# Hymba step on one core: the opening of the first projection, x issued ahead of the small loads and scale and shift formed one channel tile at a time

## The chip, the core and the metric

The kernel runs on one core of a Trainium2 chip. A core has a matrix engine (PE), a vector engine (DVE), an activation engine (ACT), a general engine (POOL) and a synchronisation engine (SP) that here only issues transfers. PE writes its results to PSUM, of which this kernel has eight banks of 128 x 512 float32. Transfers run on 16 DMA engines, shared by the queues of SP, ACT and POOL.

The metric is device time in microseconds (us) of the whole program; the median of repeated runs is compared. The span of a profile is measured inside one execution and is a little shorter than that execution's device time.

## The reference

One transformer-like layer on 128 context tokens and 256 latent tokens of width 2048, in float32. What matters here is its first step:

```python
mod = silu(cond) @ ada_w + ada_b            # cond: c_ctx for the context, c for the latents
shift_a, scale_a, gate_a, shift_f, scale_f, gate_f = 6 parts of mod
h = rmsnorm(x, norm_w[0]) * (1 + scale_a) + shift_a
q, k, v, o, g, u = split(h @ w_in)          # width 4*1024 + 32 + 1024
```

After it come a bidirectional mLSTM and a pooling mixer, an output projection, and a squared-ReLU MLP. None of that is touched by the change.

## The kernel before

**Tiling.** The 384 tokens are three blocks of 128. The 2048 channels are 16 tiles of 128, and `h` is kept transposed, channels on partitions: tile `k` of `h` is `hh`, `hl` (the high and the low part of a float32 number, split so that three fast products replace one slow one). `x` is loaded as tokens on partitions (`xtok`, three transfers of 1 MB), and each channel tile is transposed by PE into a bank `xt` and copied to the SBUF tile `xT`, by ACT for odd `k` and DVE for even `k` (`transpose_x`, L399).

**First projection.** The loop of L481 runs over eight steps `s` of two channel tiles each, and in each step over five column chunks: `u` (two of 512 columns), `v` (384, 384, and 256 with the 32 gate columns). A chunk's weights are one transfer `raw`, split by ACT into `hi` (L134) and by DVE into `lo` (L135). A chunk takes three PSUM banks, one per token block, and 18 matmuls: two channel tiles, three blocks, three products (hi x hh, hi x hl, lo x hh). At step 0 the chunk `u` of columns 0 to 511 runs its products one kind after the other, over both channel tiles. After a chunk its three banks are copied out (L514) or added up (L516).

**Scale and shift.** `mod` comes from rows of `ada_w`, streamed through PE: `ada_mat` (L239) loads 512 KB slabs `ada_raw` and multiplies them by the silu of the conditioning vectors (`sg`, transposed as `cT`, L105 to L112); ACT copies the result to `ada_sb` (L268), PE turns it to channels on partitions (L272), DVE adds the bias and the norm weight (`ada_finish`). For channel tiles 0 and 1, scale and shift are one result of 256 columns each, four slabs each. The generator `first_ada` yields between slabs; `X_ORDER` (L417) interleaves it with the first transposes and with the broadcast of 1/rms (letter `b`: `dg_rx` on DVE, `bc_rx` on PE, `rbc` on DVE); `ADA_STEPS` says how many of its slabs follow each chunk of step 0. `make_h` (L436) forms `hm` (x times scale times 1/rms) on DVE, then `hh` on ACT and `hl` on DVE.

**1/rms.** ACT squares each token block in two halves with a running sum (`junk`, L388), behind the table load and the exponential of the silu (L108); then DVE, POOL and DVE make `rx`.

**What sets the order.** Up to the first projection the order on PE, DVE and ACT is that of the code (`manual_schedule`); in the loop it is so for PE alone, and DVE, ACT and SP take an order from the planner. Each transfer of SP and ACT takes the next of eight semaphores, `DMAHW0` to `DMAHW7`, and is issued only once the transfer that had this semaphore before has landed. Tiles are reused from pools: `ada` and `hi`/`lo` have four buffers each, `raw` three, and PSUM eight banks, so that an instruction that writes a buffer waits for the last reader of what lay there.

Of the kernel before, what the change touches and what calls it, by code (L numbers as in the profile page):

```python
# [13 lines left out]
P = 128  # L14
# [29 lines left out]
def hymba_kernel(  # L44
# [6 lines left out]
    nc = tc.nc  # L51
# [24 lines left out]
    pre = pre_scope.enter_context(tc.tile_pool(name="pre", bufs=1))  # L76
    prm = pre.tile([P, 2, P], F32, name="prm")
    masks = vp.tile([P, N_CST - 3, P], F32, name="masks")
    nc.scalar.dma_start(cc[:, 0, :], c_ctx.rearrange("(p j) -> p j", j=16))
    nc.scalar.dma_start(cc[:, 1, :], c[0].rearrange("(p j) -> p j", j=16))  # L80
    nc.scalar.dma_start(cst[:, 0:3], cs_src[:, 0:3])

    vsb = [vp.tile([P, NH, 129], F32, name=f"v{i}") for i in range(3)]
    gsb = vp.tile([P, 3, 32], F32, name="gsb")
    x_tok = [pre.tile([P, D], F32, tag=f"x{i}", name=f"xtok{i}") for i in range(3)]
    for t, src in zip(x_tok, (x_prompt[0], x_sample[0, 0:128], x_sample[0, 128:256])):
        nc.sync.dma_start(t, src)
    nc.scalar.dma_start(prm[0:96, 1, :], ada_b[0].rearrange("(r p) -> r p", p=P))
    nc.scalar.dma_start(prm[0:64, 0, :], norm_w[0].rearrange("i (k p) -> (i k) p", p=P))
    nc.scalar.dma_start(prm[64:72, 0, :], mlstm_norm_w[0].rearrange("(k p) -> k p", p=P))  # L90
    nc.scalar.dma_start(prm[72:80, 0, :], pool_scale[0].rearrange("(k p) -> k p", p=P))
# [299 lines left out]
    xT = []  # L391
# [7 lines left out]
    def transpose_x(k, later=False):  # L399
        ps = bank(f"xt_{k}")  # L400
        for i in range(3):
            nc.tensor.transpose(ps[:, i * P:(i + 1) * P], x_tok[i][:, k * P:(k + 1) * P], ident)
        t = slot(f"xT{k}")
        xT.append(t)

        def copy():
            if k % 2:
                nc.scalar.activation(t[:, 0:NTOK], ps[:, 0:NTOK], AF.Copy)
            else:
                nc.vector.tensor_copy(t[:, 0:NTOK], ps[:, 0:NTOK])  # L410

        if later:
            xt_late.append(copy)
        else:
            copy()
# [20 lines left out]
    def make_h(s, between=None):  # L436
        ts = []
        for k in range(ksteps[s][0], sum(ksteps[s])):
            t, hi, lo = slot(f"hm{k}"), slot(f"hh{k}", F32R), slot(f"hl{k}", F32R)
            ts.append((k, t, hi, lo))  # L440
            for g, (a, b) in enumerate(GROUPS):
                nc.vector.scalar_tensor_tensor(t[:, a:b], xT[k][:, a:b], mod[:, 1, k, g:g + 1], rbc[:, a:b], op0=ALU.mult, op1=ALU.mult)
        if between is not None:
            between()
        for k, t, hi, lo in ts:
            for g, (a, b) in enumerate(GROUPS):
                i1 = nc.scalar.activation(hi[:, a:b], t[:, a:b], AF.Identity, bias=mod[:, 0, k, g:g + 1])
# [17 lines left out]
    w_first = load_chunk(0, 0, later=lo_later)  # L465

    def shift_rows():
        for _ in range(2):
            transpose_x(len(xT), True)
        next(ada0)  # L470
        for _ in range(2):
            transpose_x(len(xT), True)

    h_ins = make_h(0, shift_rows)
    lo_later[0]()
    for copy in xt_late:
        copy()
    order.close()
    order2 = ExitStack()
    order2.enter_context(tc.manual_schedule(engines={mybir.EngineType.PE}))  # L480
    for s in range(NS):  # L481
        for ci, (kind, c0, w) in enumerate(chunks):
            k0, nk = ksteps[s]
            hi, lo, n = w_first if s == 0 and ci < 2 else load_chunk(s, ci, h_ins if s == 0 else ())
# [3 lines left out]
            acc = [bank(f"{kind}_{c0}_{s}_{i}") for i in range(3)]  # L488

            ways = ((0, 0), (1, 0), (0, 1))  # L490
            for ps in [ways[n:n + 1] for n in range(3)] if s == ci == 0 else [ways]:
                for k in range(nk):
                    for i in range(3):
                        for a, b in ps:
                            nc.tensor.matmul(acc[i][:, 0:n], h[k0 + k][a][:, i * P:(i + 1) * P], (hi, lo)[b][:, k, :],  # L495
                                             start=k == 0 and a + b == 0, stop=k == nk - 1 and b == 1)
                    if ci == 3 and k == 0:
                        next(ada0, None)
            if s == ci == 0:
                w_first = load_chunk(0, 1, h_ins)  # L500
            if s == 0 and ci == XT_AT:
                while len(xT) < KT:
                    transpose_x(len(xT))
            for _ in range((ADA_STEPS if s == 0 else (1, 1, 1, 0, 0))[ci]):
                next(ada0, None)
            if ci == 3 and s < NS - 1:
                make_h(s + 1)
# [881 lines left out]
```

## Time and profile before

| | us |
|---|---|
| median of 3 runs | 1687.03 (1686.95, 1687.03, 1689.38) |
| device time of the profiled execution | 1689.57 |
| span in its profile | 1687.9 |
| PE busy in the span | 1656.9 (98%) |
| first matmul of the projection | 28.71 after the span's start |

In the tables of stages each row is a stretch of the span, with the busy time of each engine, the granted clock of PE, the share of the DMA engines' time and their rate. In the timelines a row is a start, a duration, an engine, a line and an operation, and in brackets how long the engine had been idle and what ended that. `SPq` and `ACTq` are the engines' instruction queues as issuers of transfers. `q1` is SP's DMA queue, `q10` that of ACT, `q0` that of POOL; their rows give packets, MB and the share of 16 engines' time.

### The profile page before, as it was taken

What the parts mean: (1) busy time and instruction counts of PE and PEld (TensorE: products, weight loads), DVE (VectorE), ACT (ScalarE), POOL (GpSimd) and SP (SyncE); (2) the same over time, 40 slices, a digit from 0 to 9 for tenths busy, and PEclk for the clock granted to TensorE, in tenths of its full rate; (3) what the DMA queues carried; (4) which work ended last, traced back from release to release, by engine and by line L of the source; (5) the groups of instructions that cost most, each with busy time, mean ns of one, the idle gap of its engine ahead of it and who ended that gap; (6) DMA issues with size and microseconds to landing.
All of it is one profiled execution on the core that took longest, in us unless ns stands there. A gap on an engine that the chain in (4) does not pass through costs nothing.

```text
span 1687.9 us, 27859 instructions
## 1 busy us (share of the span) xinstructions
PE 1656.9 (98%) x10965; PEld 1582.5 (94%) x10965; DVE 1340.3 (79%) x2009; ACT 752.4 (45%) x1225; POOL 130.9 (8%) x181
## 2 busy tenths in 40 slices
PE   6999999999999999999999999999999999999997
PEld 4888999999999989989999999999999999999996
DVE  3677769898999959997797688988588488588688
ACT  4332355555443345543444444444444444444443
POOL 0000002221000024430000000000000000000120
PEclk9999999999999999999999999999999999999999
DMA  9999857777789964754546245544344443433653
GB/s 319 316 296 298 277 160 256 238 250 223 237 270 309 311 203 129 217 153 126 173 152 194 88 138 173 158 150 140 110 150 127 124 138 114 149 122 112 187 183 134
DMA packets 258195, 320.95 MB, mean 190 GB/s; under 512 B 14752, under 2 KB 223248, under 8 KB 257680
## 3 DMA queue, kind: packets, MB, share of 16 engines
q1 hardware_dynamic: 250256, 303.41, 57.0%
q0 software_dynamic: 5856, 13.69, 2.8%
q10 hardware_dynamic: 1952, 2.07, 0.4%
q8 instruction: 86, 1.41, 0.3%
q14 instruction: 45, 0.37, 0.1%
HBM read 308.61 MB, written 10.51 MB: 189 GB/s over the span
## 4 chain that ended last, share of the span: by engine, by line
PE 90%; DVE 4%; DMA 3%; issue 1%; SPq 1%; ACT 0%; POOL 0%; DVEq 0%; ACTq 0%; POOLq 0%
PE acc_w L144 10%; PE acc_w L143 10%; PE acc_w L145 10%; PE y L1223 4%; PE y L1224 4%; PE y L1222 4%; PE v L495 4%; PE u L495 3%; PE acc_wo L143 3%; PE acc_wo L144 3%; PE acc_wo L145 3%; PE y_yz L1223 2%; PE y_yz L1222 2%; PE y_yz L1224 2%; PE y L1066 2%; PE y L1065 2%
## 5 line engine op out<-in xcount | busy, mean ns | idle before, releaser
L144 PE MATMUL acc_w<-h2l,hi_w 128*128 128x384 f32 (+1 forms) x1024 | 346.2, 338 | 0.5 <-DVE h2l L1016 0.5
L143 PE MATMUL acc_w<-h2h,hi_w 128*128 128x384 f32 (+1 forms) x1024 | 344.2, 338 | 1.2 <-ACT h2h L1012 1.2
L145 PE MATMUL acc_w<-h2h,lo_w 128*128 128x384 f32 (+1 forms) x1024 | 345.1, 337 | 0.0
L135 DVE TENSOR_TENSOR lo_w<-raw_w,hi_w 128x1024 fp32r<-128x1024 f32 x152 | 185.3, 1221 | 137.0 <-ACT hi_w L134 136.8
L134 ACT ACTIVATE hi_w<-raw_w 128x1024 fp32r<-128x1024 f32 x152 | 160.8, 1058 | 215.2 <-PE acc_w L144 94.9
L316 DVE SCALAR_TENSOR_TENSOR ada_acc<-ada_raw,sg,ada_acc 128x1024 f32<-128x1024 f32 (+1 forms) x240 | 252.0, 1080 | 0.8 <-DMA ada_raw<-in_ada_w_dram 0.7
L143 PEld LDWEIGHTS acc_w<-h2h,hi_w 128*128 128x128 f32 x1024 | 192.2, 188 | 2.8 <-ACT h2h L1012 2.0
L144 PEld LDWEIGHTS acc_w<-h2l,hi_w 128*128 128x128 f32 x1024 | 192.6, 188 | 1.2 <-DVE h2l L1016 0.8
L145 PEld LDWEIGHTS acc_w<-h2h,lo_w 128*128 128x128 f32 x1024 | 192.4, 188 | 0.3 <-DVE lo_w L135 0.2
L1208 ACT ACTIVATE hi_t<-w 128x1024 fp32r<-128x1024 f32 x104 | 109.6, 1060 | 119.1 <-DVE w L1244 34.3
L1209 DVE TENSOR_TENSOR lo_t<-w,hi_t 128x1024 fp32r<-128x1024 f32 x104 | 126.3, 1220 | 15.1 <-ACT hi_t L1208 14.8
L1209 DVE TENSOR_TENSOR lo_b<-w,hi_b 128x1024 fp32r<-128x1024 f32 x78 | 95.3, 1221 | 41.9 <-ACT hi_b L1208 41.6
L1208 ACT ACTIVATE hi_b<-w 128x1024 fp32r<-128x1024 f32 x78 | 82.5, 1059 | 98.1 <-PE acc_w L144 66.7
L134 ACT ACTIVATE hi_wo<-raw_wo 128x1024 fp32r<-128x1024 f32 x32 | 34.0, 1064 | 80.6 <-DMA raw_wo<-in_w_out_dram 57.4
L942 ACT ACTIVATE z<-acc_w 128x384 f32<-128x384 f32 x54 | 26.3, 487 | 75.1 <-PE acc_w L145 75.1
L495 PE MATMUL v<-hi_v,hh 128*128 128x384 f32 (+1 forms) x144 | 48.0, 333 | 0.0
L134 ACT ACTIVATE hi_v<-raw_v 128x768 fp32r<-128x768 f32 (+1 forms) x24 | 19.0, 793 | 64.4 <-DMA raw_v<-in_w_in_dram 55.6
L495 PE MATMUL v<-lo_v,hh 128*128 128x384 f32 (+1 forms) x144 | 46.6, 324 | 1.0 <-DVE lo_v L135 1.0
L495 PE MATMUL v<-hi_v,hl 128*128 128x384 f32 (+1 forms) x144 | 46.5, 323 | 0.0
L135 DVE TENSOR_TENSOR lo_wo<-raw_wo,hi_wo 128x1024 fp32r<-128x1024 f32 x32 | 38.8, 1217 | 7.8 <-ACT hi_wo L134 7.0
L143 PE MATMUL acc_k<-hh,hi_k 128*128 128x384 f32 x128 | 44.2, 345 | 0.0
L143 PE MATMUL acc_o<-hh,hi_o 128*128 128x384 f32 x128 | 43.9, 343 | 0.0
(2264 smaller groups left out, 4549.0 us busy)
## 6 DMA issues: line engine op xcount, KB each, us to landing
raw_w<-in_w_dram SPq DMA_DIRECT2D x152, 512.0 KB, 4.2
ada_raw<-in_ada_w_dram SPq DMA_DIRECT2D x130, 512.0 KB, 4.7
w<-in_w_dram SPq DMA_DIRECT2D x104, 512.0 KB, 4.1
raw_wo<-in_w_out_dram SPq DMA_DIRECT2D x32, 512.0 KB, 5.1
u<-in_ada_w_dram SPq DMA_DIRECT2D x18, 512.0 KB, 6.6
raw_u<-in_w_in_dram SPq DMA_DIRECT2D x16, 512.0 KB, 7.0
raw_q<-in_w_in_dram SPq DMA_DIRECT2D x16, 512.0 KB, 4.8
raw_k<-in_w_in_dram SPq DMA_DIRECT2D x16, 512.0 KB, 4.9
```

Of the source, the lines that this page charges most:

```text
L134: nc.scalar.activation(hi[:, 0:n], raw[:, 0:n], AF.Copy)
L135: low = lambda: nc.vector.tensor_tensor(lo[:, 0:n], raw[:, 0:n], hi[:, 0:n].bitcast(F32), op=ALU.subtract)
L143: nc.tensor.matmul(ps, lh, rh, start=start, stop=False)
L144: nc.tensor.matmul(ps, lh, rl, start=False, stop=False)
L145: mm3.ins = nc.tensor.matmul(ps, ll, rh, start=False, stop=stop).ins
L316: nc.vector.scalar_tensor_tensor(acc[:, g, :], raw[:, a, :], cj, acc[:, g, :], op0=ALU.mult, op1=ALU.add)
L495: nc.tensor.matmul(acc[i][:, 0:n], h[k0 + k][a][:, i * P:(i + 1) * P], (hi, lo)[b][:, k, :], start=k == 0 and a + b == 0, stop=k == nk - 1 ...
L1208: nc.scalar.activation(hi, raw, AF.Copy)
L1209: nc.vector.tensor_tensor(lo, raw, hi.bitcast(F32), op=ALU.subtract)
L1222: nc.tensor.matmul(acc, xh, wh, start=start and j == 0, stop=False)
L1223: nc.tensor.matmul(acc, xh, wl, start=False, stop=False)
L1224: nc.tensor.matmul(acc, xl, wh, start=False, stop=stop and j == 3)
```

## The change

Four things are done.

1. The three `x` transfers stand ahead of everything else. ACT's queue then issues `cst` (identity, ones), `c_ctx` and `c`, in this order; the four `prm` transfers (bias and norm weights) move from ACT's queue to POOL's.
2. For channel tiles 0 and 1, scale and shift are formed one tile at a time: scale of tile 0, shift of tile 0, then scale and shift of tile 1. Each is a result of 128 columns with two slabs of 8 x 128 (512 KB as before, in pieces of 512 B instead of 1024 B).
3. `u`'s two chunks of step 0 take tile 0's products alone (9 matmuls each), by kind; then, after tile 1's scale and shift, tile 1's. The two chunks' six banks stay open between.
4. `X_ORDER` makes 7 transposes before the first product instead of 12 (with those inside `make_h`); 5 come before tile 1's products and 4 after them. `ADA_STEPS` changes from (4, 0, 4) to (3, 2, 3).

```diff
-XT_AT = 0
-ADA_STEPS = (4, 0, 4, 0, 0)
-X_ORDER = "tatatatattaatabata"
+ADA_STEPS = (3, 2, 3, 0, 0)
+X_ORDER = "ttatatabata"
...
-    nc.scalar.dma_start(cc[:, 0, :], c_ctx.rearrange("(p j) -> p j", j=16))
-    nc.scalar.dma_start(cc[:, 1, :], c[0].rearrange("(p j) -> p j", j=16))
-    nc.scalar.dma_start(cst[:, 0:3], cs_src[:, 0:3])
...
     for t, src in zip(x_tok, (x_prompt[0], x_sample[0, 0:128], x_sample[0, 128:256])):
         nc.sync.dma_start(t, src)
-    nc.scalar.dma_start(prm[0:96, 1, :], ada_b[0].rearrange("(r p) -> r p", p=P))
...
+    nc.scalar.dma_start(cst[:, 0:3], cs_src[:, 0:3])
+    nc.scalar.dma_start(cc[:, 0, :], c_ctx.rearrange("(p j) -> p j", j=16))
+    nc.scalar.dma_start(cc[:, 1, :], c[0].rearrange("(p j) -> p j", j=16))
+    nc.gpsimd.dma_start(prm[0:96, 1, :], ada_b[0].rearrange("(r p) -> r p", p=P))
...
             if k0 == 0:
-                yield from ada_mat([(1, k0, nk)])
-                yield from ada_mat([(0, k0, nk)], ("lo",))
+                for k in range(nk):
+                    yield from ada_mat([(1, k, 1)])
+                    yield from ada_mat([(0, k, 1)], ("lo",))
...
+    def shift_rows(before, behind, later):
+        for _ in range(before):
+            transpose_x(len(xT), later)
+        next(ada0)
+        for _ in range(behind):
+            transpose_x(len(xT), later)
+
+    def chunk_mm(acc, n, w, k0, ks, nk, by_way):
+
+        ways = ((0, 0), (1, 0), (0, 1))
+        for ps in [ways[m:m + 1] for m in range(3)] if by_way else [ways]:
+            for k in ks:
+                for i in range(3):
+                    for a, b in ps:
+                        nc.tensor.matmul(acc[i][:, 0:n], h[k0 + k][a][:, i * P:(i + 1) * P], w[b][:, k, :],
+                                         start=k == 0 and a + b == 0, stop=k == nk - 1 and b == 1)
+                yield
+
     lo_later = []
...
-    h_ins = make_h(0, shift_rows)
+    w_first = [load_chunk(0, 0, later=lo_later)]
+    h_ins = make_h([0], lambda: shift_rows(1, 1, True))
     lo_later[0]()
...
+    w_first.append(load_chunk(0, 1, h_ins))
+    acc_first = []
+    for ci in range(2):
+        kind, c0, w = chunks[ci]
+        acc_first.append([bank(f"{kind}_{c0}_0_{i}") for i in range(3)])
+        for _ in chunk_mm(acc_first[ci], w, w_first[ci], 0, [0], 2, True):
+            pass
+        for _ in range(2 if ci == 0 else 3):
+            next(ada0)
+        if ci:
+            h_ins = make_h([1], lambda: shift_rows(3, 2, False))
     for s in range(NS):
         for ci, (kind, c0, w) in enumerate(chunks):
...
+            acc = acc_first[ci] if early else [bank(f"{kind}_{c0}_{s}_{i}") for i in range(3)]
+            for k, _ in enumerate(chunk_mm(acc, n, (hi, lo), k0, [1] if early else range(nk), nk, early)):
+                if ci == 3 and k == 0:
+                    next(ada0, None)
+            if s == 0 and ci == 1:
                 while len(xT) < KT:
                     transpose_x(len(xT))
```

Three places show what moves. The first is SP's queue at the program's start, before:

```order
L87 DMA xtok0_89<-in_x_prompt_dram 128x2048
L87 DMA xtok1_90<-in_x_sample_dram 128x2048 [waits DMAHW0_49]
L87 DMA xtok2_91<-in_x_sample_dram 128x2048 [waits DMAHW1_49]
L252 DMA ada_raw_1_0_0_146<-in_ada_w_dram 128x4x256 [waits DMAHW2_49]
L252 DMA ada_raw_1_0_4_158<-in_ada_w_dram 128x4x256 [waits DMAHW3_49]
```

and with the change:

```order
L82 DMA xtok0_86<-in_x_prompt_dram 128x2048
L82 DMA xtok1_87<-in_x_sample_dram 128x2048
L82 DMA xtok2_88<-in_x_sample_dram 128x2048
L250 DMA ada_raw_1_0_0_152<-in_ada_w_dram 128x8x128
L250 DMA ada_raw_1_0_8_168<-in_ada_w_dram 128x8x128
L250 DMA ada_raw_0_0_0_195<-in_ada_w_dram 128x8x128 [waits DMAHW0_49]
```

The second and third `x` transfer and the first slabs no longer wait for a small load's semaphore. The second place is ACT at the same time, before (`cc` holds `c_ctx` and `c`, `sg` is the silu's exponential, `junk` the squares of `x`):

```order
L79 DMA cc<-in_c_ctx_dram 128x16
L80 DMA cc<-in_c_dram 128x16
L81 DMA cst<-in_consts_dram 128x384
L108 ACT_TABLE_LOAD [waits DMAHW2_49]
L108 ACTIVATE sg<-cc 128x32 [waits DMAHW0_49]
L388 ACTIVATE junk,ssq<-xtok_89 128x1024 [waits DMAHW1_49]
```

and with the change:

```order
L83 DMA cst<-in_consts_dram 128x384
L84 DMA cc<-in_c_ctx_dram 128x16
L85 DMA cc<-in_c_dram 128x16
L106 ACT_TABLE_LOAD [waits DMAHW3_49]
L106 ACTIVATE sg<-cc 128x32 [waits DMAHW2_49]
L387 ACTIVATE junk,ssq<-xtok_86 128x1024 [waits DMAHW1_49]
```

The table load and the squares stand behind `cc` in both; `cc` now stands behind `cst` in ACT's queue. The third place is PE around the transposes that come between products, the first matmul of each tile shown. Before, behind the last product of `u`'s first chunk:

```order
L495 MATMUL u_0_0_2_312<-lo_u_0_0_259,hh1_267 128x512
L402 MATMUL xt_12_337<-cst_72,xtok0_89 128x128 [waits PE_49]
L402 MATMUL xt_13_343<-cst_72,xtok0_89 128x128 [waits Activation_49]
L402 MATMUL xt_14_349<-cst_72,xtok0_89 128x128 [waits DVE_49]
L402 MATMUL xt_15_355<-cst_72,xtok0_89 128x128 [waits Activation_49]
```

and with the change, behind tile 0's products of both chunks:

```order
L477 MATMUL u_512_0_2_304<-lo_u_512_0_264,hh0_235 128x512
L401 MATMUL xt_7_345<-cst_72,xtok0_86 128x128 [waits DVE_49]
L401 MATMUL xt_8_351<-cst_72,xtok0_86 128x128 [waits Activation_49]
L401 MATMUL xt_9_357<-cst_72,xtok0_86 128x128 [waits DVE_49]
L401 MATMUL xt_10_365<-cst_72,xtok0_86 128x128 [waits DVE_49]
L401 MATMUL xt_11_371<-cst_72,xtok0_86 128x128 [waits Activation_49]
L477 MATMUL u_0_0_0_267<-hi_u_0_0_231,hh1_341 128x512 [waits Activation_49]
```

Nine transposes now stand behind the first product instead of four, while six of the eight banks hold `u`'s sums.

More of the change, by code (lines that the diff above doesn't have):

```diff
@@ L87, in hymba_kernel @@
         nc.sync.dma_start(t, src)
[L88 to L91 removed]
+    nc.scalar.dma_start(cst[:, 0:3], cs_src[:, 0:3])
+    nc.scalar.dma_start(cc[:, 0, :], c_ctx.rearrange("(p j) -> p j", j=16))
+    nc.scalar.dma_start(cc[:, 1, :], c[0].rearrange("(p j) -> p j", j=16))
+    nc.gpsimd.dma_start(prm[0:96, 1, :], ada_b[0].rearrange("(r p) -> r p", p=P))
+    nc.gpsimd.dma_start(prm[0:64, 0, :], norm_w[0].rearrange("i (k p) -> (i k) p", p=P))
+    nc.gpsimd.dma_start(prm[64:72, 0, :], mlstm_norm_w[0].rearrange("(k p) -> k p", p=P))
+    nc.gpsimd.dma_start(prm[72:80, 0, :], pool_scale[0].rearrange("(k p) -> k p", p=P))
     gbias = const.tile([P, 32], F32, name="gbias")
@@ L434, in hymba_kernel, with make_h @@
     chunks = [("u", 0, 512), ("u", 512, 512), ("v", 0, 3), ("v", 3, 3), ("v", 6, 2)]
-    def make_h(s, between=None):
+    def make_h(ks, between=None):
         ts = []
-        for k in range(ksteps[s][0], sum(ksteps[s])):
+        for k in ks:
             t, hi, lo = slot(f"hm{k}"), slot(f"hh{k}", F32R), slot(f"hl{k}", F32R)
@@ L462, in load_chunk @@
         return load_w(pieces, f"{kind}_{c0}_{s}", ksteps[s][1] * n, after, later) + (n,)
-    lo_later = []
[L465 to L472, printed above, removed]
-    h_ins = make_h(0, shift_rows)
+    def shift_rows(before, behind, later):
[7 more added lines that the diff above has]
+        for ps in [ways[m:m + 1] for m in range(3)] if by_way else [ways]:
+            for k in ks:
+                for i in range(3):
[3 more added lines that the diff above has]
+                yield
+    lo_later = []
+    w_first = [load_chunk(0, 0, later=lo_later)]
+    h_ins = make_h([0], lambda: shift_rows(1, 1, True))
     lo_later[0]()
@@ L483, in hymba_kernel @@
             k0, nk = ksteps[s]
-            hi, lo, n = w_first if s == 0 and ci < 2 else load_chunk(s, ci, h_ins if s == 0 else ())
+            early = s == 0 and ci < 2
+            hi, lo, n = w_first[ci] if early else load_chunk(s, ci, h_ins if s == 0 else ())
             if s == NS - 1 and ci == 4:
@@ L487, in hymba_kernel @@
                     nc.sync.dma_start(masks, cs_src[:, 3:N_CST])
[L488 to L501, printed above, removed]
+            acc = acc_first[ci] if early else [bank(f"{kind}_{c0}_{s}_{i}") for i in range(3)]
[3 more added lines that the diff above has]
+            if s == 0 and ci == 1:
                 while len(xT) < KT:
@@ L506, in hymba_kernel @@
             if ci == 3 and s < NS - 1:
-                make_h(s + 1)
+                make_h(range(ksteps[s + 1][0], sum(ksteps[s + 1])))
             for i in range(3):
```

## The prediction

> **What bounds the kernel now.** The page first: PE is busy for nearly the whole span, so time is won or lost where PE stands still or gets work that used to lie in a gap.
>
> ```profile
> span 1687.9 us, 27859 instructions
> ...
> PE 1656.9 (98%) x10965; PEld 1582.5 (94%) x10965; DVE 1340.3 (79%) x2009; ACT 752.4 (45%) x1225; POOL 130.9 (8%) x181
> ```
>
> Then the busy time by stage (stretch, its length, PE, PEld, DVE, ACT, POOL, clock, DMA share, GB/s). The change lies in the first 60 us.
>
> ```profile
> 0.00:10.00 10.00, 0.97 (x3) 0.47 (x3) 2.09 (x10) 3.66 (x6) 2.59 (x11) 1.00 0.74 231
> 10.00:20.00 10.00, 5.41 (x35) 2.27 (x35) 1.34 (x4) 5.12 (x10) 0.89 (x1) 1.00 1.05 367
> 20.00:30.00 10.00, 9.31 (x82) 5.42 (x80) 5.29 (x15) 4.93 (x11) 0.00 (x0) 1.00 1.08 358
> 30.00:40.00 10.00, 10.00 (x74) 7.38 (x73) 6.50 (x9) 5.89 (x11) 0.00 (x0) 1.00 0.99 322
> 40.00:50.00 10.00, 10.00 (x80) 8.61 (x79) 2.42 (x8) 6.08 (x12) 0.00 (x0) 1.00 1.05 344
> ```
>
> PE idles 14 us in the first 20 us and none from 30 to 50. The chain of waits says what the idle time is for, and what PE then does without a gap (start, length, what).
>
> ```profile
> 0.80 5.19 DMA cc<-in_c_ctx_dram
> ...
> 6.01 0.33 SPq L87
> ...
> 18.73 8.55 DMA raw_u<-in_w_in_dram
> ...
> 28.71 4.63 PE u L495 x18
> 33.34 1.31 PE xt L402 x12
> 34.65 1.97 PE ada L256 x32
> 36.62 4.39 PE u L495 x18
> 41.01 3.16 PE v L495 x18
> ...
> 47.82 0.34 PE ada L272 x4
> ```
>
> The second x transfer waits until 6.0 for the semaphore of `c_ctx`; all else queues behind it in one stream, and the first product starts at 28.71. Until then PE does twelve transposes and eight slabs of scale and shift in time that it had to wait anyway. Behind 28.71 every microsecond of PE work counts. PE's later waits up to 200 us are few:
>
> ```profile
> PE v L495 <- DVE lo_v L135: 1.0, 1, 1.0
> PE ada L272 <- ACT ada_sb L268: 0.8, 1, 0.8
> ```
>
> **The change, first part: when the first product starts.** x no longer waits, but the small loads now share the DMA engines with three x transfers instead of one. Two stretches of 1 us each, at 2.5 and 3.5, show how they share (packets, MB, share):
>
> ```profile
> q1 hardware_dynamic: 35, 0.29, 72.9%
> q10 hardware_dynamic: 35, 0.00, 2.3%
> ...
> q1 hardware_dynamic: 50, 0.41, 97.0%
> q10 hardware_dynamic: 49, 0.00, 3.4%
> ```
>
> One packet of ACT's queue passes for each 8 KB packet of x, about 3 per engine and us. Before, `c_ctx` and `c` were first in ACT's queue and x had one transfer. Now the queue holds `cst`, `c_ctx`, `c`: 8 data packets and a closing one per engine each, 27 in all, and the three x transfers have as many. So `c` lands about with the last of x. Each x takes 2.6 us (in the rows below ACT begins the second at 11.35 and the third at 13.94); issued from 0.81 on without a gap, the last lands near 12.0 where it was 13.9: my estimate, first x at 5.8 as now (issue 0.81, 5.0 to landing), two more at 2.6, and 1.0 for the small packets between them. `c` lands at 12.0 too, where ACT had it at 6.29. On ACT the table load and the exponential wait for `c`, and the squares of x stand behind them:
>
> ```profile
> 6.29 1.28 ACT L108 ACT_TABLE_LOAD   x1 [6.29 <-DMA cc<-in_c_dram]
> 7.59 0.23 ACT L108 ACTIVATE sg<-cc 128x32 f32<-128x32 f32 x1
> 7.72 1.04 ACT L388 ACTIVATE junk<-xtok 128x1024 f32<-128x1024 f32 x1
> ...
> 11.35 1.06 ACT L388 ACTIVATE junk<-xtok 128x1024 f32<-128x1024 f32 x1 [1.32 <-DMA xtok<-in_x_sample_dram]
> ...
> 13.94 1.06 ACT L388 ACTIVATE junk<-xtok 128x1024 f32<-128x1024 f32 x1 [0.25 <-DMA xtok<-in_x_sample_dram]
> ...
> 16.08 0.19 ACT L388 ACTIVATION_READ_ACCUMULATOR junk<-xtok 128x1 f32 x1
> ```
>
> Before, squares ran while x arrived and ended at 16.27. Now all six come after `c`: 12.0, plus 1.4 for table and exponential (6.29 to 7.72), plus three times 2.33 (13.94 to 16.27) is 20.4, 4.1 later. What follows, with its rows:
>
> ```profile
> 16.30 0.16 DVE L394 TENSOR_REDUCE ss<-ssq 128x3 f32<-128x6 f32 x1 [7.12 <-ACT junk L388]
> 16.57 0.55 DVE L410 COPY xT<-xt 128x384 f32<-128x384 f32 x1
> 17.50 0.49 ACT L408 ACTIVATE xT<-xt 128x384 f32<-128x384 f32 x1 [1.23 <-PE xt L402]
> 19.68 0.55 PE L402 MATMUL xt<-cst,xtok 128*128 128x128 f32 x3
> 23.50 0.55 DVE L206 TENSOR_TENSOR dg_rx<-cst,rx 128x384 f32<-128x384 f32 x1
> 24.10 0.91 PE L208 MATMUL bc_rx<-dg_rx,cst 128*128 128x384 f32 x2 [0.49 <-DVE dg_rx L206]
> 26.76 0.38 ACT L268 ACTIVATE ada_sb<-ada 128x256 f32<-128x256 f32 x1 [0.17 <-PE ada L256]
> 27.31 1.06 ACT L134 ACTIVATE hi_u<-raw_u 128x1024 fp32r<-128x1024 f32 x1 [0.17 <-DMA raw_u<-in_w_in_dram]
> 28.27 1.48 ACT L447 ACTIVATE hh<-hm,mod 128x128 fp32r<-128x128 f32 x4
> ```
>
> DVE stands in order: sum and scale 0.3, two copies 1.0 (both waited for nothing but the squares ahead of them in DVE's queue), scale of tile 0 0.4, `dg_rx` 0.55: 22.7. `bc_rx` 0.9: 23.6. PE has tile 0's shift behind it: two slabs of 0.5 (1.97 for four), a transpose 0.33 (1.31 for four), 0.3 until the last is through: 25.2. `ada_sb` 0.3, then on ACT `hi_u` 1.06 and the first `hh` 0.3, with hand-overs of 0.05 (`dg_rx` ends 24.05, `bc_rx` starts 24.10): 27.6. `raw_u` is no longer what ends last: 12.0 plus four slabs of 1.75 (a price from below) plus 1.4 is 20.4. So the first product starts at 27.6 instead of 28.71: **-1.1**, where the x transfers alone promised more. Lower bound: `c` as early as before, 21.9 (rival A). Upper bound: if `c` also waits for the first two slabs, 3.5 later, 31.1.
>
> The Trainium skill, "TensorE: Matmul & The Clock Gate", Part 1, says that an idle window of about 3.4 us halves the array's clock until it has been busy as long. PE would idle from about 16 to 21 here, while it waits for ACT behind the squares. Nothing in the rows quoted shows PE after such a gap; by the page's halving, the two slabs and the transpose (1.33 us) would take about 1.3 more, and the sum below would be +8.4 instead of +7.1, an estimate.
>
> **Second part: PE work that now stands behind the first product.** Tile 1's four slabs 1.97, two more turns of the result (L272, 0.34 for four records, 0.17 each) 0.34, and five more transposes (nine instead of four) at 0.33, 1.65. Together **+3.96**. The products themselves are the same 36 matmuls. A slab now has eight matmuls of 128 columns instead of four of 256; below, each costs half: no change; above, each costs as much as one of 256: +2.0. I take the lower: 18 products of 512 columns took 4.39, 18 of 384 took 3.16, so time goes with the columns.
>
> **Third part: PE waits that arise.** The sums of `u` hold six banks from the first product to the copies after tile 1, scale or shift holds a seventh, and one is left for transposes. So each transpose waits until the one before is copied out: 0.55 until it is through, 0.53 copy (ACT 0.49, DVE 0.55), two hand-overs, 1.18, of which PE works 0.33: 0.85 idle. That meets transposes 8 and 9 in full, 10 by half (0.4, a turn stands between), and 13, 14, 15 in full: 4.65. Transpose 11's copy stands on ACT ahead of tile 1's `hh`: 0.9 before tile 1's first product. Tile 0's third kind of product waits for `lo_u`, which DVE makes behind `hl`: 0.8 for `hl` and 1.2, against 1.4 for six products: 0.5. Together **+6.05**. Below: none of it if work fills the gaps, but PE's order is the code's, so nothing can step forward; I allow 3. Above, with a second ACT item ahead of each copy, 9.
>
> **Fourth part: what is given back.** At step 1 and 4 PE waits 1.0 and 0.8 for late weights; PE coming later, both should vanish: **-1.8**. The work behind is unchanged in PE's order.
>
> Cost nothing: `prm` on POOL (needed first at 21, by `ada_finish`), the reversed `cst` (first transposes wait for x), the number of slabs.
>
> **Sum:** -1.1 + 3.96 + 6.05 - 1.8 = +7.1. The profiled execution took 1689.57 around its span of 1687.9, and would take 1696.7; the median of the runs shown is 1687.03, 2.5 lower, so I predict 1694.1.
>
> **Rivals.** *A, the small loads are not held back.* `c` lands at 6.3; squares end 2.4 after x, and `raw_u` sets the start: 20.4 + 1.06 + 0.3 and hand-overs, 21.9, 5.7 earlier than forecast. PE then reaches the second slab of tile 1's shift at 28.3, which lands at 30.3 (four slabs, two `raw_u`, and one slab of 1.5 further down the stream), and waits 2.0. 7.1 - 5.7 + 2.0 = +3.4: 1690.4. For it: in the trace `c_ctx` needed 5.2 us beside one x. Against: the rows of 35 to 35 and 50 to 49.
>
> *B, transfers in 512 B pieces are slow.* Bounds from stretches at 6.1 to 6.5 (mostly the small loads' 512 B) and 13.5 to 15.5 (1024 B):
>
> ```profile
> q10 hardware_dynamic: 188, 0.08, 72.6%
> ...
> q1 hardware_dynamic: 751, 0.75, 108.3%
> ```
>
> 0.726 x 16 x 0.4 us / 188 is 25 ns a packet of 0.4 KB on average, and 1.083 x 16 x 2 / 751 is 46 ns for 1 KB. I take 27 ns, 64 per engine and slab, 1.75 us. At 46 a slab takes 2.9; six slabs later the second slab of tile 1's shift lands at about 40 where PE is at 34: +5.8, 1699.9.
>
> *C, not slower: the transfers, not PE, set step 1.*
>
> ```profile
> 62.55 0.45 PE L495 MATMUL v<-lo_v,hh 128*128 128x384 f32 x1 [1.02 <-DVE lo_v L135]
> ```
>
> At 62.55 PE restarts when the late weights of step 1's `v` are split. Those weights land as before: the stream starts 1.9 earlier, and eight slabs at 0.25 more take 2.0. If PE reaches that chunk by then, nothing is lost: 1687.1. It needs PE to be at most 1.0 late there, so the waits for copies would have to cost nothing and tile 1's work lie in a gap. For it: the DMA share of about 1 from 10 to 50. Against: only 1.0 us of PE's wait hangs on it.
>
> **How the numbers follow.** Forecast 0.70, A 0.14, B 0.08, C 0.08. A measurement of this kernel tells about 0.2%, 3.4 us, from no change. C gives 0.03 to faster and 0.05 to the same; half of A, at the edge, counts as the same, 0.07; the rest is slower: 0.03, 0.12, 0.85. The range takes A's foot and B: 1689.5 to 1700.
>
> **What would show it.** ACT's table load at about 12 instead of 6.29; squares without a pause until 20.4; the first product near 27.6; transposes of step 0 in single groups of three with ACT or DVE copies between them; step 1's chunks without a wait for weights, about 8 later than now. A table load near 6 would make part one wrong, transposes in one run part three, a restart at 62.5 the whole.

## The result, and the profile after

The changed kernel takes **1700.56 us** (median of 5 runs, 1699.80 to 1704.00) beside 1687.03 for the kernel before: 1.0077 times, with a 95% interval of 1.0066 to 1.0087. It is slower, as forecast, but by 13.5 us and not by 7.1. Its profiled execution took 1699.80 around a span of 1698.1, 10.2 more than that of the kernel before. The head of its page:

```profile
span 1698.1 us, 28009 instructions
...
PE 1660.7 (98%) x11029; PEld 1586.1 (93%) x11029; DVE 1341.7 (79%) x2012; ACT 750.9 (44%) x1227; POOL 133.6 (8%) x185
```

PE's busy time in the whole span grew by only 3.8 us (1656.9 before), so 6.4 of the 10.2 are time in which it stands still. The stages of the changed kernel (stretch, length, PE, PEld, DVE, ACT, POOL, granted clock, DMA share, GB/s) say where:

```profile
10.00:20.00 10.00, 4.78 (x43) 2.89 (x42) 1.22 (x6) 5.85 (x10) 0.00 (x0) 1.00 1.13 318
20.00:30.00 10.00, 6.41 (x48) 3.58 (x48) 3.73 (x12) 4.13 (x11) 0.89 (x1) 1.00 0.96 282
30.00:40.00 10.00, 8.59 (x93) 5.87 (x91) 4.89 (x11) 3.53 (x8) 0.00 (x0) 1.00 0.85 262
40.00:50.00 10.00, 8.29 (x51) 5.90 (x52) 4.60 (x8) 3.82 (x7) 0.00 (x0) 0.83 0.48 152
50.00:60.00 10.00, 8.06 (x66) 5.52 (x64) 2.32 (x3) 6.01 (x12) 0.00 (x0) 1.00 0.95 312
```

From 30 to 60 PE was busy for all but 0.07 of 30 us before; now it idles 5.1 there. And from 40 to 50 the granted clock is 0.83 on the mean, where it had been 1.00. The chain of waits (start, length, what), from the small loads to step 1:

```profile
1.73 12.23 DMA cc<-in_c_dram
...
14.04 1.28 ACT L106
...
24.61 1.65 PE bc_rx L206 x2
26.25 1.01 PE ada L254 x16
27.27 0.83 PE xt L401 x3
28.10 1.06 PE ada L254 x16
...
33.82 1.01 PE ada L254 x32
...
38.77 0.50 ACT xT L407
...
39.32 0.56 PE xt L401 x3
...
39.90 0.57 DVE xT L409
...
43.25 3.77 PE u L477 x9
...
48.45 2.27 PE u L477 x9
```

`c` lands at 14.01. Ahead of the first product, 16 records of a slab take 1.01 (26.25); behind it, 32 records of the same kind take 1.01 (33.82). Nine products of 512 columns take 3.77 at 43.25 and 2.27 at 48.45. The same work runs at two speeds. Between 38.8 and 43.2 the chain goes back and forth between single transposes and their copies.

The first product starts at 30.80 (28.71 before), `v`'s first chunk of step 0 at 55.50 (40.84), step 1 at 66.7 (52.05), step 2 at 88.03 (75.25). The distance is 2.09, 14.66, 14.65 and 12.78 there, and 10.2 at the end. Set beside the forecast:

| term | forecast | profile |
|---|---|---|
| first product (part 1) | -1.1 | +2.1 |
| from there to `v`'s first chunk (parts 2 and 3) | +10.0 | +12.6 |
| given back later (part 4) | -1.8 | -4.5 |
| sum, profiled executions | +7.1 | +10.2 |
| from the profiled executions to the medians | 0 | +3.3 |

### The profile page after: what moved, and what is told of

The parts are those of the page before. It is cut to its first block, busy times and chain, and to the rows that moved or that the text cites. A ratio compares the mean times of both kernels' runs of the same rounds, so it can differ in the third digit from the quotient of the medians.

```text
span 1698.1 us, 28009 instructions
## 1 busy us (share of the span) xinstructions
PE 1660.7 (98%) x11029; PEld 1586.1 (93%) x11029; DVE 1341.7 (79%) x2012; ACT 750.9 (44%) x1227; POOL 133.6 (8%) x185
## 4 chain that ended last, share of the span: by engine, by line
PE 90%; DVE 5%; DMA 2%; issue 2%; ACT 1%; POOL 0%; ACTq 0%; DVEq 0%; SPq 0%; POOLq 0%
PE acc_w L141 10%; PE acc_w L142 10%; PE acc_w L143 10%; PE y L1235 4%; PE y L1236 4%; PE y L1234 4%; PE v L477 4%; PE u L477 4%; PE acc_wo L141 3%; PE acc_wo L142 2%; PE acc_wo L143 2%; PE y_yz L1235 2%; PE y_yz L1234 2%; PE y_yz L1236 2%; PE y L1077 2%; PE y L1076 2%
```

## Experiments

All were timed beside fresh runs of the kernel before, whose medians in the three series were 1688.71, 1687.89 and 1688.56. "Way" is the time from the first product to `v`'s first chunk of step 0; "half clock" is the time behind the first product, up to 60, in which the records of the granted clock show 0.50. First product, way and half clock are those of one profiled execution, whose time was not always near the median: 1688.18 for `one_cc_bias`, 1707.50 for `warm`.

| kernel | median | ratio to before (95%) | first product | way | half clock |
|---|---|---|---|---|---|
| before | 1687.03 | 1 | 28.7 | 12.1 | 0 |
| changed | 1700.56 | 1.0077 (1.0066 to 1.0087) | 30.8 | 24.7 | 3.4 |
| after_again | 1699.19 | 1.0060 (1.0046 to 1.0074) | 30.5 | 25.0 | 3.4 |
| cc_first | 1699.15 | 1.0061 (1.0048 to 1.0074) | 24.5 | 29.5 | 13.7 |
| spread | 1698.36 | 1.0056 (1.0043 to 1.0070) | 30.5 | 19.6 | 0 |
| warm | 1705.73 | 1.0100 (1.0086 to 1.0114) | 28.8 | 27.1 | 10.2 |
| order_only | 1689.33 | 1.0006 (0.9997 to 1.0015) | 30.5 | 12.0 | 0 |
| one_chunk | 1694.38 | 1.0036 (1.0024 to 1.0049) | 31.0 | 19.3 | 0 |
| cc_spread | 1693.24 | 1.0030 (1.0018 to 1.0043) | 25.1 | 21.0 | 3.4 |
| order_cc | 1687.30 | 0.9993 (0.9985 to 1.0002) | 28.6 | 12.0 | 0 |
| bias_late | 1697.93 | 1.0062 (1.0049 to 1.0076) | 29.3 | 24.7 | 3.4 |
| order_bias | 1686.80 | 0.9990 (0.9981 to 0.9998) | 27.3 | 12.0 | 0 |
| one_cc_bias | 1691.98 | 1.0018 (1.0009 to 1.0028) | 26.2 | 19.3 | 0 |
| tile_only | 1695.24 | 1.0047 (1.0033 to 1.0062) | 26.5 | 24.8 | 3.4 |

The theory to be tested: three things make the loss, (1) the late `c`, (2) the transposes' wait for copies in the one free bank, (3) PE's clock, which is at half where PE has stood still. Each has a rival in its expectation.

### The two parts of the change apart

`order_only` is the kernel before with the new order of the loads alone:

```
 for t, src in zip(x_tok, ...):
     nc.sync.dma_start(t, src)
+nc.scalar.dma_start(cst...); (cc, c_ctx); (cc, c)     # were ahead of x
+nc.gpsimd.dma_start(prm...)                           # was nc.scalar
```

> The kernel before with only the first part of the change: x issued ahead, cst, c_ctx, c behind it on ACT, prm on POOL; scale and shift of both tiles at once as before. c lands at 14.0 and squares end at 22.5, as in the changed kernel. Theory (most of the loss is the tile-wise scheme): the first product comes 0 to 1.5 later than 28.7, the total 1686.5 to 1689. Rival (most of the loss is the late c): first product 3 to 5 later, the total 1690 to 1693.

```profile
13.74 1.28 ACT L108 ACT_TABLE_LOAD   x1 [13.74 <-DMA cc<-in_c_dram]
...
29.00 1.05 ACT L134 ACTIVATE hi_u<-raw_u 128x1024 fp32r<-128x1024 f32 x1
30.07 1.09 ACT L447 ACTIVATE hh<-hm,mod 128x128 fp32r<-128x128 f32 x3
```

These rows of ACT's timeline have `c` at 13.74 and `hi_u` at 29.00 without a wait for its data (27.31, with one, before). The first product comes 1.8 later and the total is 1689.33, both 0.3 above what was expected; by its interval the total is the same as before. The new order of the loads, late `c` included, costs little by itself: 0.6 of the medians. That this is because the slabs and `raw_u` keep PE and DMA occupied until 27 in the old scheme anyway is my reading; no run shows it.

`tile_only` is the changed kernel with the loads of the kernel before:

```
+nc.scalar.dma_start(cc, c_ctx); (cc, c); (cst)        # ahead of x, as before
 for t, src in zip(x_tok, ...):
     nc.sync.dma_start(t, src)
-nc.gpsimd.dma_start(prm...)
+nc.scalar.dma_start(prm...)
```

> The changed kernel with the loads of the kernel before (c_ctx, c, cst first, x's second transfer behind c_ctx, prm on ACT): the tile-wise scheme alone. c lands at 6.3, squares end at 16.3, raw_u sets the first product near 23. From there the waits of the changed kernel, 24.7 to v's first chunk, and 1 to 3 more for tile 1's slabs, which come late for so early a start: 49 to 51 beside 40.8 before; total 1695 to 1698. Rival (the scheme is good and the loads spoil it): total at or below 1688.

It has the first product 2.2 earlier than the kernel before, at 26.5 where I expected 23, and loses 12.7 more on the way. `raw_u` does not set its start: `hi_u` begins at 25.15 without a wait for its data, and PE is at half speed until 24.6 (`bc_rx` takes 1.65 at 20.45). It ends at 1.0047, inside the expected total. So the tile-wise scheme alone brings 6.7 us and the new order of the loads alone 0.6, of the 11.3 to 13.5 that both bring together. The new order costs the changed kernel 4.3 at the first product (30.8 against 26.5), more than twice the 1.8 that it costs in the old scheme.

### The late small loads

`cc_first` puts `c_ctx` and `c` ahead of `cst` on ACT's queue:

```
-nc.scalar.dma_start(cst...); (cc, c_ctx); (cc, c)
+nc.scalar.dma_start(cc, c_ctx); (cc, c); (cst...)
```

> The changed kernel with one edit: on ACT's queue c_ctx and c go ahead of cst. Theory 1 (the late c sets the first product): c's packets are the first 18 instead of the last 18 of 27 per engine, so c lands near 10 instead of 14.0; table load near 10, squares until about 18.4 instead of 22.5, first product between 25 (if PE's clock is full by then) and 26.7, instead of 30.8; the total 4 to 6 lower, 1694.5 to 1696.5. Rival (slabs or raw_u set the start, the late c is hidden): the table load comes at 10 as well, but the first product stays within 1 us of 30.8 and the total within 1 us of 1700.6.

The table load comes at 9.53 and the first product at 24.49, 6.3 earlier: the late `c` did set the start, and `raw_u` did not. But the total falls by 1.4 at most, not by 4 to 6. The expectation missed because the way got 4.8 longer: 1.4 are waits for tile 1's slabs, which land late for so early a start (rival A had 2.0 for this), and the rest I put down to the half clock, 13.7 us instead of 3.4. Two stretches of `cc_first` show how the clock falls (columns as above), the second right behind the first:

```profile
31.77:35.19 3.42, 1.82 (x30) 1.00 (x22) 0.34 (x1) 0.77 (x2) 0.00 (x0) 1.00 1.05 338
35.19:38.60 3.41, 2.44 (x12) 2.18 (x11) 1.03 (x3) 0.49 (x1) 0.00 (x0) 0.50 1.09 360
```

`bias_late` asks why `c` came at 14.0 and not at 12.0 as forecast. It issues the load of `gate_bias` to all partitions on POOL behind the scale of x:

```
-nc.gpsimd.dma_start(gbias, gate_bias... .partition_broadcast(P))
 ...
+with tc.issue_after(rstd_cols(rx, ss, 3, 1.0 / D).ins):
+    nc.gpsimd.dma_start(gbias, gate_bias... .partition_broadcast(P))
```

> The changed kernel with one edit: the load of gate_bias to all partitions is issued on POOL behind the scale of x (near 24) instead of at 3.6. If its sixteen 1 KB packets, which take 0.2 to 1.5 us each near 8.7, are what holds x and c back: the stretch 8 to 10 keeps 350 GB/s or more instead of 233, the last x lands near 12.9 instead of 13.8, c near 13 instead of 14.0, the first product near 29.8 instead of 30.8; the total 1 lower, within what can be told. Rival (those packets only wait for their turn behind x's): the same landings within 0.2.

The queues in the stretch from 8 to 10 (packets, MB, share of 16 engines), first in the changed kernel:

```profile
q1 hardware_dynamic: 70, 0.44, 57.7%
q0 software_dynamic: 75, 0.02, 46.3%
```

and in `bias_late`:

```profile
q1 hardware_dynamic: 111, 0.78, 94.8%
q0 software_dynamic: 111, 0.01, 4.1%
```

What follows on ACT's timeline in `bias_late`:

```profile
12.58 1.28 ACT L105 ACT_TABLE_LOAD   x1 [12.58 <-DMA cc<-in_c_dram]
```

0.02 MB of POOL's queue took 46.3% of the DMA engines' time for 2 us. Without `gate_bias` it takes 4.1%, x's queue moves 0.78 MB instead of 0.44, `c` lands 1.5 earlier and the first product comes 1.5 earlier, at 29.35, a little more than the 1.0 expected. By the medians that can't be told from no gain. So 1.5 of the 2.0 by which my landing of `c` was off were the packets of `gate_bias`, which the forecast had left out altogether.

### PE's clock

`warm` fills PE's gap ahead of the first product with 20 transposes of the identity that nobody reads:

```
-X_ORDER = "ttatatabata"
+X_ORDER = "ttatat1a2bata"
...
+    idle = bank("idle")
...
+        if op in "12":
+            for _ in range(12 if op == "1" else 8):
+                nc.tensor.transpose(idle[:, 0:P], ident, ident)
```

> The changed kernel with 20 idle transposes of the identity into a spare bank (12 ahead of the first turn of the result, 8 behind it), work that nobody reads: it bridges PE's gap from 20.4 to 24.6. Theory 3 (PE's clock stays at half because PE is idle there): bc_rx takes 0.9 instead of 1.65, the two slabs behind it 0.5 each instead of 1.0, the transposes 0.12 each instead of 0.24; the first product comes about 2 us earlier, at 28.7, and the total is about 2 lower, 1698.5. Rival (these rows are slow for another reason, the fp32 weights or the bank): the rows keep their length and the total stays at 1700.6 or rises by up to 1.

PE's timeline in the changed kernel:

```profile
18.51 1.08 PE L254 MATMUL ada<-ada_raw,cT 128*32 128x128 f32 x16
...
24.61 1.65 PE L206 MATMUL bc_rx<-dg_rx,cst 128*128 128x384 f32 x2 [0.91 <-DVE dg_rx L204]
```

and in `warm`:

```profile
18.51 1.08 PE L254 MATMUL ada<-ada_raw,cT 128*32 128x128 f32 x16
...
24.61 0.91 PE L206 MATMUL bc_rx<-dg_rx,cst 128*128 128x384 f32 x2 [0.19 <-DVE dg_rx L204]
25.45 0.65 PE L254 MATMUL ada<-ada_raw,cT 128*32 128x128 f32 x16
26.03 0.55 PE L401 MATMUL xt<-cst,xtok 128*128 128x128 f32 x3
...
28.84 1.13 PE L481 MATMUL u<-hi_u,hh 128*128 128x512 f32 x3 [0.47 <-ACT hh L450]
```

`bc_rx` starts at the same 24.61 and takes 0.91 instead of 1.65; a slab takes 0.65 as the timeline counts it, where the one at 18.51 took 1.08; the first product comes 1.96 earlier. So 2.0 of the delay at the first product was PE's clock. The gap did not lower it: the slab at 18.51, ahead of the gap, takes 1.08 in both kernels. It kept the clock from rising. The total went the other way, to 1.0100. Behind the first product `warm` has more half clock, 10.2 us. The planner's order on ACT, DVE and SP beyond step 0 had also moved with the added work, and a wait of 1.74 at 149, in step 4, was followed by another half-clock stretch there. By the starts of the steps `warm` lies 0.5 behind the changed kernel at `v`'s first chunk, 1.4 at step 4 and 4.9 at step 5. How much each of these adds to the total I can't say, so `warm` settles the clock ahead of the first product and nothing behind it.

`after_again` is the changed kernel once more:

> The changed kernel once more, unedited, beside the runs of the kernel before on this chip. If half-clock stretches depend on where PE's waits fall on the clock's own windows, their number or length behind the first product differs from the first profile (43.0 to 46.4), while the waits between transposes are the same; the total lies 11 to 15 above the kernel before. Rival (the clock follows from the work alone): the stretch lies at the same place with the same length.

The half clock came at 43.3 to 46.7, 0.3 from its first place, and the waits were the same. The expectation that it would move was wrong, though the run tests it little: the borders of the clock's windows lay only 0.37 from where they had been. The ratio, 1.0060, is lower than in the first series: the two series put the loss at 13.5 and 11.3 us, the two profiled spans at 10.2 and 10.7.

### The waits for copies

`spread` places the nine transposes of step 0 singly between `u`'s groups of three products; `one_chunk` leaves them in their runs and lets only `u`'s first chunk go by tile, so that `u`'s second chunk does not yet hold three banks:

```
 # spread
...
-for _ in chunk_mm(acc_first[ci], ..., [0], 2, True):
-    pass
+for m, _ in enumerate(chunk_mm(acc_first[ci], ..., [0], 2, True)):
+    if m != 1:
+        transpose_x(len(xT))
 # and likewise between tile 1's groups; one is left for shift_rows
 # one_chunk
-for ci in range(2):
+for ci in range(1):          # u's first chunk alone by tile
...
-early = s == 0 and ci < 2
+early = s == 0 and ci < 1
```

> The changed kernel with the nine transposes of step 0 that stand in runs of five and four put singly between the groups of three products of u's two chunks. Theory 2 (runs of transposes wait for each other's copies in the one free bank): the waits of 0.6 between transposes, 4.5 us of PE in all, shrink below 1.5, the half-clock stretch at 43.0 to 46.4 goes, and v's first chunk of step 0 starts about 19 us behind the first product instead of 24.7; the total 4 to 6 lower, 1694.5 to 1696.5. Rival (late weights would stop PE anyway): what is won is lost in waits for slabs or weights before step 1's second half, and the total stays within 2 us of 1700.6.

> The changed kernel, but only u's first chunk takes tile 0's products alone; u's second chunk takes both tiles as before, so that its three banks are free while the nine transposes run, in the same runs of five and four. Theory 2 (one free bank is the cause): the transposes follow each other without the waits of 0.6, no half-clock stretch behind the first product, v's first chunk starts 17 to 18.5 us behind the first product instead of 24.7; the total 5 to 7 lower than the changed kernel. Rival (the copies themselves are too slow, whatever the banks): the waits stay, and so does the total within 2 us.

The stretch from the first product to `v`'s first chunk, in the kernel before, in the changed kernel and in `one_chunk`:

```profile
28.71:40.84 12.13, 12.13 (x80) 8.91 (x81) 7.74 (x12) 7.92 (x15) 0.00 (x0) 1.00 1.00 323
```

```profile
30.80:55.50 24.70, 20.16 (x171) 13.65 (x171) 10.44 (x19) 8.15 (x17) 0.00 (x0) 0.93 0.73 234
```

```profile
31.00:50.30 19.30, 17.74 (x173) 12.65 (x172) 10.25 (x19) 10.78 (x21) 0.00 (x0) 1.00 0.88 274
```

PE's idle time is 0, 4.54 and 1.56; its busy time 12.13, 20.16 and 17.74. In `one_chunk` the same transposes run without a break, as its chain of waits shows:

```profile
36.88 1.13 PE xt L401 x9
38.01 0.12 PE ada L270 x2
38.13 0.73 PE xt L401 x6
...
42.24 1.31 PE xt L401 x12
```

Five transposes take 1.86 and four take 1.31, where the changed kernel needed one copy between any two. The way falls by 5.4, a little less than expected (19.3, not 17 to 18.5), and the total by 4.8 against `after_again`, 0.2 short of the range. `spread` brings the same way, 19.6, but a total only 0.8 lower than `after_again`, where 4 to 6 was expected: behind it the wait for step 1's weights is there again (1.3 at 70.8), so that of the 5.4 gained at `v`'s first chunk 3.4 are left where step 7 ends, and a half-clock stretch at 552 falls into its profile. Its rival was right in kind.

`cc_spread` joins `cc_first` and `spread`; `one_cc_bias` joins `cc_first`, `one_chunk` and `bias_late`:

> Both mends in one, c_ctx and c ahead of cst, and the nine transposes spread between u's products. If late c and copy waits are the two causes, and half-clock stretches follow from the waits: first product near 24.5, no half-clock stretch behind it, v's first chunk near 45 (19.6 for the way between, 1 for a slab that is late), 4 later than in the kernel before; total 1691 to 1693. Rival (weights of step 1 stop PE however early it comes): PE waits 2 us or more in step 1, and the total is that of spread alone, 1698.

> The tile-wise scheme with all its side costs mended: u's first chunk alone by tile, c_ctx and c ahead of cst, gate_bias late. First product near 24, v's first chunk 19 to 21 behind it (19.3 with one chunk, and up to 1.5 for tile 1's slabs, which land late for so early a start), 44 to 45 beside 40.8 before; total 1690.5 to 1692.5: the scheme's own work behind the first product costs about what the earlier start brings, so it stays above the kernel before. Rival (the scheme wins once its waits are gone): below 1688.

`cc_spread` came out 0.2 above its range, with 3.4 of half clock where none was expected and 1.3 of wait for weights in step 1; `one_cc_bias` came out inside its range. The latter has the way of `one_chunk`, 19.3, from a start at 26.2; 24 was expected, but PE's clock was at half until 25.2 there, and full from 18.1 in `cc_first`, with the same work ahead of the first product. With these three mends the scheme still ends 0.18% (0.09 to 0.28%) above the kernel before by the medians: it starts 2.5 earlier and has 7.2 more on the way. Its profile, of an execution of 1688.18, can't show the whole of this: it lies 4.7 behind the kernel before at `v`'s first chunk and 2.0 where step 7 ends, and its span is 1.4 shorter.

### The loads alone, mended

`order_cc` and `order_bias` take the kernel before with x ahead, `prm` on POOL and `c_ctx`, `c`, `cst` in the old order, the second also with `gate_bias` late (edits as above).

> The kernel before with x issued ahead, prm on POOL, and c_ctx, c, cst on ACT in the old order. c lands at 9.5 and squares end near 18, so that raw_u sets the first product, which comes about 1.5 to 2 us earlier than 28.7 since the stream starts that much earlier. If PE's work behind the first product is the bound, the total is 1 to 2 lower than before, 1686.5 to 1688 beside 1688.7; if step 1's late weights are, the gain is lost in that wait and the total is the same within 1 us.

> The kernel before with x ahead, c_ctx and c ahead of cst, prm on POOL, and gate_bias behind the scale of x. The last x lands near 13, raw_u near 26 instead of 27.3, the first product near 27.6 instead of 28.7; if the packets of gate_bias held the stream. If PE's work behind it is the bound, the total is 1 to 2 lower than before, 1686 to 1687 beside 1688; if step 1's late weights are, the same within 0.5.

In `order_cc` the first product is only 0.1 earlier, where 1.5 to 2 was expected, since `gate_bias` holds the stream, and `raw_u` lands at 27.15. In `order_bias` `raw_u` no longer ends last. ACT's timeline there:

```profile
25.80 1.05 ACT L133 ACTIVATE hi_u<-raw_u 128x1024 fp32r<-128x1024 f32 x1
26.86 1.49 ACT L447 ACTIVATE hh<-hm,mod 128x128 fp32r<-128x128 f32 x4
```

and PE's waits from 30 to 130 (what waits, for what, us in total, times, longest):

```profile
PE ada L271 <- ACT ada_sb L267: 1.5, 1, 1.5
PE v L495 <- DVE lo_v L134: 1.3, 1, 1.3
```

The first product starts 1.4 earlier, and PE's two later waits grow from 0.8 and 1.0 to 1.5 and 1.3. The medians give 1.8 us less than before, 0.10% with an interval of 0.02 to 0.19%. This is the one version whose interval lies below the kernel before. The gain is less than the 0.2% of the forecast's bound, and one such interval among twelve runs is weak evidence.

## Why the prediction was right or wrong

**Which steps failed.** `c`'s landing was put at 12.0 without the load of `gate_bias`, and it landed at 14.0. PE's clock was left out of the sum on both sides of the first product, and it cost 2.0 ahead of it and 1.5 behind it. The step from the profiled executions to the medians was put at nothing, and it was 3.3.

**Direction and rivals.** Slower was right, and the kind of waits was right: single transposes with ACT or DVE copies between them, no wait for weights at step 1. Rival A did not happen; `c` was later even than I thought. Rival C did not happen: step 1 had no wait left, and the time was not the old one. Rival B did not happen either. x's queue in the changed kernel from 13.5 to 15.5, where the kernel before moved 0.75 MB:

```profile
q1 hardware_dynamic: 1190, 0.60, 120.9%
```

Pieces of 512 B are slower, by a fifth here, but PE waits for no slab between 30.8 and 55.5. The measured 1700.56 lies 6.5 above the predicted time and 0.6 above the range. In the profiled executions the sum was 3.1 too low, and that is partly luck: parts 1 to 3 were 5.8 too low, and part 4 gave back 2.7 more than forecast.

**Part 1, 3.2 too low.** The step that failed is "the last lands near 12.0 ... `c` lands at 12.0 too". x was estimated from 2.6 us each and 1.0 for small packets; `gate_bias` stood in the same stretch and was not counted (1.5 by `bias_late`). From `c` to the last square I had 8.4, and it was 8.5. For 0.5 of the landing no run shows the cause. The clock is 2.0 by `warm`. My prediction named a rule for it, worked out 1.3 and left it out of the sum. The 1.3 had only two slabs and the turn of the result in it; `bc_rx`, 0.74 longer than in `warm`, was not in it. The Trainium skill, "TensorE: Matmul & The Clock Gate", Part 1, has this rule: an idle window halves the clock until a busy one has passed. The trace agrees with its second half: the rows get short only from about 29, behind 3.41 us without a pause. Its first half did not act here, since the clock was at half already ahead of the gap; it did in `spread`, where the clock was full at 19.8, PE worked 0.57 in the next 3.41 us and the clock was at half from 23.2. Against these losses, two steps behind the squares were too long in the forecast: 0.3 up to the end of `dg_rx`, and 0.6 from there to the first product (4.9 against 4.3 in `warm`; the durations named there add up to 4.2, and hand-overs of 0.05 don't fill the rest).

**Parts 2 and 3, 2.6 too low.** Without the shortage of banks and without half clock the way is 19.3, 7.2 more than before. For this I had 5.4: 3.96 of work, 0.9 for `hh` (measured 0.87) and 0.5 for `lo_u` (0.23). Slabs and transposes have about the prices I gave (4 slabs 2.0, five transposes 1.86 against 1.65, and the 128-column matmul does cost half). Missing were a fifth slab of step 1's scale and shift that now runs ahead of `v`'s first chunk, 0.5, a wait of `one_chunk`'s own for `ada_sb`, 0.46, and slow restarts: the first three products take 1.13 after a wait, the next three 0.86. A few tenths of the 1.8 I have not taken apart. For the shortage of banks I had 4.65, and it cost 5.4. In that lies the half clock, which I had nowhere: nine products 3.77 instead of 2.27, 1.5. Without it the shortage cost about 3.9, less than forecast: the waits between transposes were 0.58 to 0.65, not 0.85, and a transpose counts 0.55 of PE's busy time where I had taken 0.33 of the 1.18 as work.

**Part 4, 2.7 too low.** The wait at step 1 was worth 1.9, not 1.0, and that at 113.6 (in step 3; the forecast called it step 4) 1.1, not 0.8. Step 1 in the kernel before and in the changed kernel:

```profile
52.05:75.25 23.20, 22.10 (x161) 17.62 (x159) 14.93 (x33) 7.42 (x13) 0.00 (x0) 1.00 0.88 286
```

```profile
66.70:88.03 21.33, 21.33 (x160) 17.85 (x159) 15.42 (x31) 8.45 (x14) 0.00 (x0) 1.00 0.88 284
```

By step 7's end 3.0 of the 4.5 are given back. PE's ends are modelled, and a wait can also hide in matmuls that look longer. Most of the other 1.5 would be a half-clock stretch of the kernel before that the changed kernel's profile doesn't have:

```profile
544.57:547.98 3.41, 3.41 (x13) 3.41 (x12) 3.32 (x7) 1.43 (x5) 0.00 (x0) 0.50 1.07 366
```

13 records stand there and 21 in the stretch behind it. Such a stretch is in some profiles and not in others: `after_again` has one at 555, the first profile of the same kernel none.

**From the profile to the median, 3.3 too low.** "the median of the runs shown is 1687.03, 2.5 lower" took three runs as the level. The changed kernel's profiled execution was 0.8 below its own median. Over the later series the kernel before has medians 0.9 to 1.7 higher than those three, and the changed kernel's second series is 11.3 above it, not 13.5. Which level is the right one for the first series stays open.

## What to carry to other kernels

Work that is split to start earlier brings only what its start was waiting for: here the start came 2.2 to 4.2 us earlier in the four versions that brought `c` early, and the split put at least 7 us of work and waits behind it. Before products that hold their banks are split, count the banks that are left for everything that is copied out in between; where one is left, each copy is a wait. And add up PE's short waits over a few microseconds, since they can also halve its clock: here, in the first 200 us, they did where PE was busy for no more than 1.91 of 3.41 us.

## What the runs showed of the hardware

**The clock falls by windows of 3.41 us, at about half busy.** All changes of the granted clock in these 14 profiles are 3.41 us or a multiple apart within a profile. Three windows of the changed kernel, cut at those times:

```profile
39.55:42.96 3.41, 1.85 (x14) 1.29 (x12) 1.27 (x3) 1.04 (x3) 0.00 (x0) 1.00 1.09 353
42.96:46.38 3.42, 3.13 (x7) 2.46 (x8) 2.67 (x4) 2.27 (x5) 0.00 (x0) 0.50 0.17 53
...
49.79:53.21 3.42, 2.19 (x14) 1.43 (x12) 0.56 (x1) 0.49 (x1) 0.00 (x0) 1.00 1.08 361
```

Up to 200 us, in all 14 profiles, every window at full clock with at most 1.91 us of PE time was followed by a half-clock window, and none with 1.95 or more; the clock came back only after windows with 3.13 or more. Windows of 3.04 (`after_again`, 16.0) and 3.13 (`one_cc_bias`, 14.9), ahead of the first record of the clock, did not yet bring it up. (Behind 200 us the rule is not this simple: the window ahead of the one at 544 has 2.67. In it stand matmuls of 4 columns; whether they count for less, no run shows.) So 1.56 of waits in one window, short ones of 0.3 to 0.7, can cost a further 1.5, and where the windows' borders lie decides whether they do. In `tile_only` the same two runs of transposes fall out the other way round, the first without and the second with a fall:

```profile
34.82:38.24 3.42, 2.07 (x14) 1.53 (x14) 0.99 (x3) 0.82 (x2) 0.00 (x0) 1.00 1.07 362
...
45.06:48.48 3.42, 1.70 (x11) 0.90 (x9) 1.00 (x2) 0.49 (x1) 0.00 (x0) 1.00 1.03 336
48.48:51.89 3.41, 3.24 (x21) 1.64 (x22) 0.11 (x1) 2.73 (x6) 0.00 (x0) 0.50 0.82 281
```

The Trainium skill, "TensorE: Matmul & The Clock Gate", Part 1, gives the window as 3413 ns, with which the runs agree, and speaks of an idle window; here 1.85 of 3.41 busy was idle enough. The same page of the Trainium skill, in its section "A second HAM failure mode: psum-queue depth-cycling", says that small idle times between groups of matmuls make the clock swing, and this is what the runs of transposes did. Until the first change of the clock in a profile the stage table shows 1.00 although the work runs at half speed (a slab 1.08 at 18.51 in `warm`, 0.65 at 25.45), so that there only the lengths of the rows tell.

**A small load can hold the DMA engines for long, depending on what runs beside it.** With the 16 packets of 1 KB of `gate_bias` POOL's queue took 46.3% of 16 engines for 2 us, against 4.1% without them: nearly 0.9 us each, beside x with its packets of 8 KB. In `bias_late` the same 16 packets, at 26.2 to 26.8 beside the slabs, took 0.05 us each, as other packets of 1 KB in the kernel before (46 ns). What makes the difference stays open.
